# A decoder layer on one core: projections in tiles of 512 tokens, entry normalisation on VectorE alone, stores of normalised tiles moved from SyncE's queue to ScalarE's

## The chip, the cores and the metric

One core of a Trainium2 chip runs the whole program. The metric is the device time of one execution in microseconds (us); lower is better. The engines are TensorE (PE in the rows, its weight loads PEld), VectorE (DVE), ScalarE (ACT), GpSimd (POOL) and SyncE (SP), which here only issues transfers. Each engine takes its instructions in order, and so does each queue of transfers: what stands behind a waiting instruction waits too.

## What is computed

One post-norm decoder layer on 1024 tokens of width 1024, cut to its steps:

```python
h = layer_norm(x, ln_in_g, ln_in_b)                      # entry
proj = h @ w_in                                          # q, k, v of both head groups, 2304 columns
sb = stick_breaking_attention(q_sb, k_sb, v_sb)          # 8 heads of 64, strictly causal
sw = sliding_window_attention(q_sw, k_sw, v_sw, ...)     # 8 heads, 2 key heads, window 128, sinks
merged = concatenate([rms_norm(sb), rms_norm(sw)])
h = layer_norm(ALPHA * h + merged @ w_out, ln1_g, ln1_b)
ffn = (silu(h @ w_gate) * (h @ w_up)) @ w_down           # d_ff = 2816
out = layer_norm(ALPHA * h + ffn, ln2_g, ln2_b)
```

Inputs and outputs are float32. The result must agree with this to a small tolerance.

## The kernel before

**Products in three passes.** A float32 product is made of three matmuls in the type fp32r: each operand is split into a high part (a cast) and a low part (the operand less the cast), and `mm3` (line 178) adds high x high, high x low and low x high in one PSUM bank. So each split costs a cast on ScalarE and a subtraction, on GpSimd for weights (`split_w`, line 114), on VectorE for attention's values (`split_ps`, line 119), on TensorE by a matmul with minus the identity and a second cast for activations (`split_pe`, line 127).

**Entry.** The eight tiles of 128 tokens are loaded (`load_x`, line 263) and normalised (`norm`, line 323, through `ln_apply`, line 156): two `bn_stats` and `bn_aggr` on VectorE, the power for 1/sigma on GpSimd (`rpow`, line 141), then the scaling. Tiles 0 and 1 are scaled by VectorE alone (`fast`: one instruction of 1024 columns, line 159, and two of 512, line 162); for tiles 2 to 7 ScalarE subtracts the mean (line 169), VectorE multiplies (line 170) and GpSimd adds the offset (line 172), each in two halves. A normalised tile is stored to `h_dram` (line 330) and turned on TensorE (`turn_in`, line 332) into the split arrays `xh`, `xl`, four pairs with 256 tokens each. Between the first turns `warm` (line 317) issues 21 matmuls on the identity whose result nobody reads.

**Projections.** `xmul` (line 343) multiplies a strip of 128 weight columns with tokens. In the loop of lines 591 to 604 it runs over `c`, four pieces of 256 tokens, as the tiles arrive: keys, values, two strips of queries, and from the second piece on two blocks of the sliding-window attention (`swa_attend`). Later it takes two pieces at once (`nc_` = 2), still as two runs of 24 matmuls with 256 columns each, one after the other in one PSUM bank: 4 calls in `swa_project` (line 383), 24 in `sb_project` (line 445). Their weights come by `strip` (line 210).

**Around the last projections.** `merge` interleaves attention with projections, and later with the first half of the output projection. Then, for pairs of token tiles in the order 0, 2, 1, 3 (lines 690 to 712), `out_proj` finishes the output projection, `ln_apply` normalises the tile, line 695 stores it to `h1_dram` from SyncE's queue, and `put_b` (line 675) turns it and splits it into the right-hand arrays of the feed-forward part, which is a seven-product scheme (P1 to P7). A tile's `copied` cast is the ScalarE read of its turned data. The loads that `out_proj` needs next (`m`, line 535; `res`, line 631) and the first feed-forward weights (`gr`, `ur`, line 736) stand in SyncE's queue too.

**What sets the order.** A scheduler in the framework orders each engine's instructions from its own model of their times, under the data dependencies and a few added ones: `pe.after(a, b)` puts `a` behind `b` without a wait of its own. So an edit in one place can move instructions elsewhere.

Of the kernel before, what the change touches and what calls it, by code (L numbers as in the profile page):

```python
# [13 lines left out]
F32 = mybir.dt.float32  # L14
# [7 lines left out]
P = 128  # L22
# [59 lines left out]
def layer(ctx: ExitStack, tc: tile.TileContext, x, ln_in, w_sw, w_sb, norm_g,  # L82
# [31 lines left out]
    def split_w(raw, hi, lo):  # L114
        ins = act.copy(hi, raw)  # L115
        pool.tensor_tensor(out=lo, in0=raw, in1=_f(hi), op=ALU.subtract)  # L116
        return ins
# [9 lines left out]
    def split_pe(pending, ps, hi, lo):  # L127

        act.copy(hi, ps)

        def finish():
            pe.matmul(ps, negi, hi, start=False, stop=True, skip_group_check=True)
            act.copy(lo, ps)
        flush(pending)
        pending.append(finish)

# [4 lines left out]
    def rpow(dst, var, scale, eps):  # L141
        dve.tensor_scalar(out=var, in0=var, scalar1=scale, scalar2=eps, op0=ALU.mult, op1=ALU.add)  # L142
        pool.tensor_tensor(out=dst, in0=var, in1=mhalf, op=ALU.pow)  # L143

    def ln_stats(xt, n=2, eps=LN_EPS):
        bst = st.tile([P, n, 6], F32, tag=f"bst{n}", name="bst")
        w, first = D // n, []
        for i in range(n):
            first.append(dve.bn_stats(out=bst[:, i, :], in_=xt[:, i * w:(i + 1) * w]))  # L149
        mv = st.tile([P, 2], F32, tag="mv", name="mv")  # L150
        dve.bn_aggr(out=mv, in_=bst)  # L151
        rstd = st.tile([P, 1], F32, tag="rstd", name="rstd")
        rpow(rstd, mv[:, 1:2], 1.0, eps)
        return mv[:, 0:1], rstd, first
# [36 lines left out]
    for c in range(4):  # L191
        xh.append((c1p, rp)[c // 2].tile([P, KT, 256], F32R, tag="r", name=f"xh{c}"))
        xl.append((c1p, rp)[c // 2].tile([P, KT, 256], F32R, tag="r", name=f"xl{c}"))
# [14 lines left out]
    loaded = []  # L208

    def strip(i, ahead=2):  # L210
        while len(loaded) < min(len(strips), i + ahead):
            i_ = len(loaded)
            raw = w_raw(strips[i_])
            hi, lo = (U([P, KT, P], "whu"), U([P, KT, P], "wlu")) if i_ == 3 else w_tiles()
            for k in (slice(0, 4), slice(4, KT)) if i_ < 2 else (slice(0, KT),):
                ins = split_w(raw[:, k], hi[:, k], lo[:, k])
                if i_ == 0:
                    pe.after(ins, copied)
# [98 lines left out]
    def warm(n):  # L317

        ps = bps.tile([P, P], F32, tag="z", bufs=ZB, name="warm")
        for i in range(n):  # L320
            pe.matmul(ps, negi, negi, start=True, stop=True)

    def norm(t):
        xt = xts[t]
        first, last = ln_apply(xt, xt, g_in, b_in, t < 2)
# [6 lines left out]
    def turn_in(t):  # L332
        xt = xts.pop(t)
        c, o, todo = t // 2, (t % 2) * P, []
        for g in range(2):
# [4 lines left out]
            split_pe(todo, ps, xh[c][:, 4 * g:4 * g + 4, o:o + P], xl[c][:, 4 * g:4 * g + 4, o:o + P])  # L340
        flush(todo)

    def xmul(w, c0, nc_):
        hi, lo = w
        ps = bps.tile([P, nc_, 256], F32, tag="pp", name="pp")
        for h in range(nc_):
            mm3(ps[:, h, :], [(hi[:, k, :], lo[:, k, :], xh[c0 + h][:, k, :], xl[c0 + h][:, k, :])
                              for k in range(KT)])
        return ps.rearrange("p a b -> p (a b)"), slice(c0 * 256, (c0 + nc_) * 256)
# [223 lines left out]
    strip(0, 2)  # L573
    load_x(2)
    load_x(3)
    strip(2, 2)
    for t in range(4, NT):
        load_x(t)
# [5 lines left out]
    pe.on, pe.last = True, None  # L584
    warm(3)
    turn_in(0)
    warm(12)
    turn_in(1)
    warm(6)
    pe.on = False  # L590
# [84 lines left out]
    def put_b(name, src, o):  # L675
# [6 lines left out]
        for hi, k0 in hw:  # L682
            n = hi.shape[1]
            split_pe(todo, ps[:, k0:k0 + n], hi[:, :, o:o + P], lw[0][0][:, k0:k0 + n, o:o + P])
# [3 lines left out]
    hs = {}  # L688
    d0, d1 = slice(0, 512), slice(512, D)
    for n, c in enumerate(order):  # L690
        if n in (1, 2):
            ms[order[n + 1]] = out_load(0, order[n + 1])
        for t, h in out_proj(c, ms[c], wo, load_acc(c, acc_dram), ("z" if n < 3 else "pp", "pp")):
            ln_apply(h, h, g1, b1, True, LN_EPS / ALPHA ** 2)
            sp.dma_start(h1_dram[t], h)
            o = (t % 4) * P
            if t < 4:
                hs[t] = h
                put_b("B11", h[:, d0], o)
                put_b("B21", h[:, d1], o)  # L700
# [7 lines left out]
            put_b("B22", h[:, d1], o)  # L708
# [321 lines left out]
```

## Time and profile before

| | |
|---|---|
| Time, median of 3 runs | 1191.04 us (1190.03 to 1191.77) |
| The profiled execution | 1192.59 us, its span 1190.8 us |
| Mean granted clock of TensorE | 0.988 of full speed |
| Busy in the span: TensorE, VectorE, GpSimd, ScalarE | 96%, 70%, 52%, 49% |
| Matmuls | 6319 |
| Moved by the DMA engines | 140.17 MB, 118 GB/s on average |

The span runs from the program's first instruction to its last; 1.8 us of the execution lie around it. Busy times are shares of the whole span, over stages that differ; a matmul's record begins when it starts and overlaps the next one's, so TensorE's pace is read from the starts of matmuls that follow each other, not from their durations.

### The profile page before, as it was taken

To read this page: it belongs to the slowest core of one execution; us is meant where nothing else is said; L and a number is where in the kernel's file an instruction comes from. 1 tells how busy PE (TensorE), PEld (TensorE's weight loads), DVE (VectorE), ACT (ScalarE), POOL (GpSimd) and SP (SyncE) were. 2 spreads that over 40 slices of the span, in tenths; PEclk is the share of its full clock that TensorE was granted. 3 is DMA by queue.
4 is the path that set the end of the run, shared out by engine and by line. 5 is a ranking of instruction groups with operands and counts; after the bars stand their busy time and mean duration, and the time that the engine had idled before them with its cause. 6 is when DMAs were issued, how large, how long until landed. Compare 5 with 4: busy or idle time off the path is not lost. (4 is left out here: it accounts for less than half of the span.)

```text
span 1190.8 us, 17761 instructions
## 1 busy us (share of the span) xinstructions
PE 1147.4 (96%) x6319; PEld 989.4 (83%) x6319; DVE 836.0 (70%) x1279; ACT 584.5 (49%) x1269; POOL 622.0 (52%) x590
## 2 busy tenths in 40 slices
PE   7799999999999999988999999999999999999996
PEld 5798999999998778866878888888888888888885
DVE  6676687988888887976765546555565448899735
ACT  5566578777777754247423222233323234455531
POOL 5514234757666864334877656676567520000584
PEclk9899999999999999989999999999999999999999
DMA  8302102111104635243333323332233239853431
GB/s 272 144 16 89 32 19 77 31 50 41 50 15 142 217 119 170 106 159 138 119 115 115 107 74 121 116 111 89 84 115 122 82 124 385 328 186 104 129 124 71
DMA packets 59912, 140.17 MB, mean 118 GB/s; under 512 B 7045, under 2 KB 18862, under 8 KB 59824
## 3 DMA queue, kind: packets, MB, share of 16 engines
q1 hardware_dynamic: 45552, 111.24, 29.2%
q10 hardware_dynamic: 14272, 27.81, 6.1%
q8 instruction: 50, 0.82, 0.3%
q14 instruction: 38, 0.31, 0.1%
HBM read 95.23 MB, written 41.17 MB: 115 GB/s over the span
## 5 line engine op out<-in xcount | busy, mean ns | idle before, releaser
L116 POOL TENSOR_TENSOR w<-s,w 128x512 fp32r<-128x512 f32 x88 | 125.5, 1429 | 117.0 <-ACT w L115 117.0
L183 PE MATMUL pp<-xh,whi 128*128 128x256 f32 x544 | 158.6, 292 | 0.0
L183 PE MATMUL pp<-xl,whi 128*128 128x256 f32 x544 | 157.1, 289 | 0.0
L183 PE MATMUL pp<-xh,wlo 128*128 128x256 f32 x544 | 156.8, 289 | 0.0
L115 ACT CAST w<-s 128x512 fp32r<-128x512 f32 x88 | 54.5, 622 | 201.3 <-PE pgu L770 121.6
L843 PE MATMUL pd<-bhl,ahl 128*128 128x512 f32 x612 | 139.2, 389 | 0.0
L843 PEld LDWEIGHTS pd<-bhl,ahl 128*128 128x128 f32 x612 | 114.8, 188 | 24.2 <-DVE bhl L835 0.4
L802 DVE TENSOR_TENSOR t<-t,pgu 128x512 f32<-128x512 f32 x88 | 60.0, 682 | 97.5 <-PE pgu L770 97.3
L481 POOL TENSOR_TENSOR s<-s,s 128x127 f32<-128x127 f32 (+2 forms) x96 | 94.6, 990 | 42.6 <-DVE s L477 20.8
L183 PEld LDWEIGHTS pp<-xh,whi 128*128 128x128 f32 x544 | 106.0, 195 | 1.0 <-issue 0.2
L183 PEld LDWEIGHTS pp<-xl,whi 128*128 128x128 f32 x544 | 105.8, 195 | 0.9
L183 PEld LDWEIGHTS pp<-xh,wlo 128*128 128x128 f32 x544 | 105.5, 194 | 1.0
L835 POOL TENSOR_TENSOR ahl<-ar,ahl 128x512 fp32r<-128x512 f32 x12 | 16.2, 1354 | 134.8 <-ACT ahl L834 134.7
L477 DVE TENSOR_TENSOR_SCAN s<-s,brk 128x128 f32<-128x128 f32 (+1 forms) x64 | 72.8, 1143 | 8.8 <-ACT s L468 8.2
L120 ACT CAST at<-tra 128x256 fp32r<-128x256 f32 (+1 forms) x160 | 55.7, 357 | 44.4 <-DVE at L121 31.6
L834 ACT CAST ahl<-ar 128x512 fp32r<-128x512 f32 x63 | 39.1, 622 | 77.2 <-PE pd L843 47.9
L422 POOL TENSOR_TENSOR L<-L,rd 128x512 f32<-128x512 f32 (+1 forms) x32 | 30.9, 987 | 87.0 <-DVE rd L420 61.1
L121 DVE TENSOR_TENSOR at<-tra,at 128x256 fp32r<-128x256 f32 (+1 forms) x160 | 58.9, 381 | 10.3 <-ACT at L120 8.9
L116 POOL TENSOR_TENSOR w<-gr,w 128x512 fp32r<-128x512 f32 x44 | 62.0, 1419 | 7.6 <-ACT w L115 7.6
L770 PE MATMUL pgu<-B11h,w 128*128 128x512 f32 x176 | 57.9, 390 | 1.6 <-ACT w L115 1.0
L770 PE MATMUL pgu<-T4h,w 128*128 128x512 f32 x176 | 57.9, 390 | 1.5 <-DVE t L802 1.5
L770 PE MATMUL pgu<-T3h,w 128*128 128x512 f32 x176 | 57.9, 390 | 1.0 <-ACT w L115 1.0
(242 smaller groups left out, 3311.8 us busy)
## 6 DMA issues: line engine op xcount, KB each, us to landing
ar<-a_dram SPq DMA_DIRECT2D x73, 256.0 KB, 3.0
a_dram<-act ACTq DMA_DIRECT2D x33, 512.0 KB, 2.6
gr<-in_w_gu SPq DMA_DIRECT2D x24, 512.0 KB, 3.5
ur<-in_w_gu SPq DMA_DIRECT2D x23, 512.0 KB, 3.5
bq<-in_w_down SPq DMA_DIRECT2D x44, 256.0 KB, 5.2
raw<-in_w_sb SPq DMA_DIRECT2D x12, 512.0 KB, 3.4
m<-o_dram SPq DMA_DIRECT2D x32, 128.0 KB, 2.9
res<-h_dram SPq DMA_DIRECT2D x8, 512.0 KB, 5.8
```

What stands on the lines that cost most here:

```text
L115: ins = act.copy(hi, raw)
L116: pool.tensor_tensor(out=lo, in0=raw, in1=_f(hi), op=ALU.subtract)
L120: act.copy(hi, ps)
L121: dve.tensor_tensor(out=lo, in0=ps, in1=_f(hi), op=ALU.subtract)
L183: pe.matmul(ps, a, b, start=(i == 0), stop=(i == n - 1))
L422: pool.tensor_tensor(out=Ls[i], in0=Ls[i], in1=rd[:, 2 * i:2 * i + 2].unsqueeze(2).broadcast_to([P, 2, nk]), op=ALU.mult)
L477: dve.tensor_tensor_scan(s2[:, 0:w][:, ::-1], s2[:, 0:w][:, ::-1], brk[:, 512 - w:][:, ::-1] if last else zero.broadcast_to([P, w]), 1.0 i ...
L481: pool.tensor_tensor(out=s1[:, 0:m], in0=s1[:, 0:m], in1=s2[:, 1:m + 1], op=ALU.mult)
L770: pe.matmul(ps, a, b, start=(start and n == 0), stop=(stop and n == 11), skip_group_check=True)
L802: add = lambda out, x: dve.tensor_tensor(out=out, in0=x, in1=ps, op=ALU.add)
L834: act.copy(w[:, 0], src)
L843: pe.matmul(pd[t], x, y, start=(first and k == 0 and n == 0), stop=(end and k == KF - 1 and n == 2), skip_group_check=True)
```

## The change

It has three parts. (1) `xh` and `xl` become two groups of 512 tokens (each as two tiles of four strips of the contraction), and `xmul` with two pieces issues one run of 24 matmuls with 512 columns in place of two with 256. (2) At the entry all tiles take `ln_apply`'s VectorE form; the `warm` matmuls go; the first two weight strips are loaded ahead of the remaining tiles of `x`, all of `x` is asked for before the next strips, and the first strip's low half is put behind the power of tile 1 on GpSimd. (3) The store of a normalised tile to `h1_dram` is issued from ScalarE's queue, behind the cast of the tile's second `put_b`.

```diff
@@ split_w, split_pe, rpow return their instruction @@
     def split_w(raw, hi, lo):
         ins = act.copy(hi, raw)
-        pool.tensor_tensor(out=lo, in0=raw, in1=_f(hi), op=ALU.subtract)
-        return ins
+        return ins, pool.tensor_tensor(out=lo, in0=raw, in1=_f(hi), op=ALU.subtract)
...
-    for c in range(4):
-        xh.append((c1p, rp)[c // 2].tile([P, KT, 256], F32R, tag="r", name=f"xh{c}"))
-        xl.append((c1p, rp)[c // 2].tile([P, KT, 256], F32R, tag="r", name=f"xl{c}"))
+    for c in range(2):
+        xh.append([(c1p, rp)[c].tile([P, 4, 512], F32R, tag="r", name=f"xh{c}") for g in range(2)])
+        xl.append([(c1p, rp)[c].tile([P, 4, 512], F32R, tag="r", name=f"xl{c}") for g in range(2)])
...
-            raw = w_raw(strips[i_])
+            raw = raws0.pop(0) if raws0 else w_raw(strips[i_])
...
-                ins = split_w(raw[:, k], hi[:, k], lo[:, k])
+                cast, low = split_w(raw[:, k], hi[:, k], lo[:, k])
                 if i_ == 0:
-                    pe.after(ins, copied)
+                    pe.after(cast, copied)
+                    pe.after(low, powers[1])
...
-    def warm(n):
-
-        ps = bps.tile([P, P], F32, tag="z", bufs=ZB, name="warm")
-        for i in range(n):
-            pe.matmul(ps, negi, negi, start=True, stop=True)
-
     def norm(t):
         xt = xts[t]
-        first, last = ln_apply(xt, xt, g_in, b_in, t < 2)
+        first, last = ln_apply(xt, xt, g_in, b_in, True)
...
     def xmul(w, c0, nc_):
         hi, lo = w
-        ps = bps.tile([P, nc_, 256], F32, tag="pp", name="pp")
-        for h in range(nc_):
-            mm3(ps[:, h, :], [(hi[:, k, :], lo[:, k, :], xh[c0 + h][:, k, :], xl[c0 + h][:, k, :])
-                              for k in range(KT)])
-        return ps.rearrange("p a b -> p (a b)"), slice(c0 * 256, (c0 + nc_) * 256)
+        c, o, n = c0 // 2, (c0 % 2) * 256, nc_ * 256
+        ps = bps.tile([P, n], F32, tag="pp", name="pp")
+        mm3(ps, [(hi[:, k, :], lo[:, k, :], xh[c][k // 4][:, k % 4, o:o + n], xl[c][k // 4][:, k % 4, o:o + n])
+                 for k in range(KT)])
+        return ps, slice(c0 * 256, c0 * 256 + n)
...
-    strip(0, 2)
-    load_x(2)
-    load_x(3)
-    strip(2, 2)
-    for t in range(4, NT):
+    raws0 += [w_raw(strips[i]) for i in range(2)]
+    for t in range(2, NT):
         load_x(t)
...
     norm(0)
     norm(1)
-    pe.on, pe.last = True, None
-    warm(3)
+    strip(0, 2)
     turn_in(0)
-    warm(12)
     turn_in(1)
-    warm(6)
-    pe.on = False
+    strip(2, 2)
...
+    def store(t, h, copied):
+
+        pe.after(act.dma_start(h1_dram[t], h), copied)
+
...
             ln_apply(h, h, g1, b1, True, LN_EPS / ALPHA ** 2)
-            sp.dma_start(h1_dram[t], h)
...
-                put_b("B21", h[:, d1], o)
+                store(t, h, put_b("B21", h[:, d1], o))
...
-            put_b("B22", h[:, d1], o)
+            store(t, h, put_b("B22", h[:, d1], o))
```

**How it moves instructions.** First, GpSimd at the entry (`rstd` is the power for a tile's 1/sigma, the second one tile 1's; `wlo`, `wlu` are weights' low parts; `x` a tile of tokens). Before:

```order
L143 TENSOR_TENSOR rstd<-mv,mhalf 128x1
L286 TENSOR_SCALAR nsink<-sink 128x8
L116 TENSOR_TENSOR wlo<-raw,whi 128x512 x4
L143 TENSOR_TENSOR rstd<-mv,mhalf 128x1
L116 TENSOR_TENSOR wlo<-raw,whi 128x1024
L143 TENSOR_TENSOR rstd<-mv,mhalf 128x1
L116 TENSOR_TENSOR wlu<-raw,whu 128x1024
L172 TENSOR_TENSOR x_203<-x_203,b_in 128x512 x2
```

and now:

```order
L143 TENSOR_TENSOR rstd<-mv,mhalf 128x1
L289 TENSOR_SCALAR nsink<-sink 128x8
L143 TENSOR_TENSOR rstd<-mv,mhalf 128x1
L116 TENSOR_TENSOR wlo<-raw,whi 128x512 x4
L143 TENSOR_TENSOR rstd<-mv,mhalf 128x1 x2
L116 TENSOR_TENSOR wlo<-raw,whi 128x1024
L116 TENSOR_TENSOR wlu<-raw,whu 128x1024
L143 TENSOR_TENSOR rstd<-mv,mhalf 128x1 x4
```

The second power has moved ahead of four weight subtractions, and GpSimd's additions to `x` are gone; ScalarE's `L169` instructions are gone with them.

Second, SyncE's queue around the normalised tiles of the last stage (`h_dram_108` to `115` are the eight tiles of `h1_dram`, `m` and `res` the loads of `out_proj`, `gr` the first feed-forward weights). Before:

```order
L695 DMA h_dram_112<-res 128x1024
L695 DMA h_dram_113<-res 128x1024
L535 DMA m<-o_dram_92 128x256
L535 DMA m<-o_dram_93 128x256
L535 DMA m<-o_dram_94 128x256
L535 DMA m<-o_dram_95 128x256
L631 DMA res<-acc_dram_102 128x1024
```

and now:

```order
L622 DMA res<-acc_dram_105 128x1024
L532 DMA m<-o_dram_92 128x256
L532 DMA m<-o_dram_93 128x256
L532 DMA m<-o_dram_94 128x256
L532 DMA m<-o_dram_95 128x256
L622 DMA res<-acc_dram_102 128x1024
```

The four loads of `m` for the last piece stood behind the stores of tiles 0, 1, 4 and 5 and no longer do; in the same way the first `gr` loads stood behind those of tiles 2, 3, 6 and 7.

Third, TensorE at the turns of tiles 4 and 5 (`trh` is turned data, with `ident` a turn, with `negi` the subtraction of a high part; `pc` is the output projection). Before:

```order
L125 MATMUL trh<-ident,res 128x128 x4
L125 MATMUL trh<-ident,tt 128x128 x7
L132 MATMUL trh<-B22h,negi 128x512
L125 MATMUL trh<-ident,tt 128x128
L125 MATMUL trh<-ident,res 128x128 x4
L183 MATMUL pc<-woh,whi 128x512
L183 MATMUL pc<-wol,whi 128x512
L183 MATMUL pc<-woh,wlo 128x512
```

with nine more `pc` behind them, and now:

```order
L124 MATMUL trh<-ident,res 128x128 x4
L124 MATMUL trh<-ident,tt 128x128 x8
L124 MATMUL trh<-ident,res 128x128 x4
L131 MATMUL trh<-B22h,negi 128x512
L131 MATMUL trh<-T2h,negi 128x512 x2
L124 MATMUL trh<-ident,tt 128x128 x4
L131 MATMUL trh<-T1h,negi 128x512
L131 MATMUL trh<-T3h,negi 128x512
```

The twelve `pc` that stood among these turns have moved ahead of them; the next `pc` now come only after the turns of both tiles.

## Rows read from the trace of the kernel before

**Rows 1.** Busy time by stage (windows): stretch, length, each engine (instructions), clock, DMA, GB/s.
```profile
0.00:60.00 60.00, 46.98 (x232) 37.30 (x233) 39.70 (x76) 31.65 (x60) 35.06 (x34) 0.91 0.60 206
120.00:380.00 260.00, 258.39 (x2073) 251.01 (x2072) 213.48 (x372) 191.93 (x495) 144.16 (x197) 1.00 0.16 46
480.00:560.00 80.00, 73.07 (x362) 57.90 (x361) 62.48 (x100) 38.61 (x79) 29.66 (x25) 0.96 0.36 127
```

**Rows 2.** Timeline of PE, projections: start, duration, instruction (second: 24th after the first).
```profile
130.66 0.28 PE L183 MATMUL pp<-xh,whi 128*128 128x256 f32 x1
...
133.53 0.28 PE L183 MATMUL pp<-xh,whi 128*128 128x256 f32 x1
```

**Rows 3.** Timeline of PE, output projection (second: 13th after the first).
```profile
495.17 0.39 PE L183 MATMUL pc<-woh,wlo 128*128 128x512 f32 x1
...
498.12 0.39 PE L183 MATMUL pc<-woh,whi 128*128 128x512 f32 x1
```

**Rows 4.** Timeline of all engines, entry; in brackets idle time before, and what ended it.
```profile
7.71 1.29 DVE L159 SCALAR_TENSOR_TENSOR x<-x,mv,g_in 128x1024 f32<-128x1024 f32 x1 [1.86 <-ACT g_in L282]
...
11.96 5.94 POOL L116 TENSOR_TENSOR wlo<-raw,whi 128x512 fp32r<-128x512 f32 x4 [1.63 <-ACT whi L115]
...
13.35 0.15 DVE L142 TENSOR_SCALAR mv<-mv 128x1 f32<-128x1 f32 x1
...
17.85 0.57 POOL L143 TENSOR_TENSOR rstd<-mv,mhalf 128x1 f32<-128x1 f32 x1
18.46 1.41 DVE L162 SCALAR_TENSOR_TENSOR x<-x,rstd,b_in 128x512 f32<-128x512 f32 x2 [2.92 <-POOL rstd L143]
...
26.35 0.52 PE L183 MATMUL pp<-xl,whi 128*128 128x256 f32 x1
...
35.43 0.33 ACTq L330 DMA_DIRECT2D h_dram<-x  x1
35.80 0.37 ACT L370 COPY vr<-pp 128x256 f32<-128x256 f32 x1 [3.21 <-POOL x L172]
...
41.06 0.80 PE L132 MATMUL trx<-xh,negi 128*128 128x512 f32 x1 [4.25 <-ACT xh L129]
```

**Rows 5.** Windows of 4 us at the entry, columns as in rows 1.
```profile
34.00:38.00 4.00, 0.95 (x6) 0.32 (x4) 4.00 (x5) 0.37 (x1) 4.00 (x3) 0.80 0.32 131
...
42.00:46.00 4.00, 4.00 (x21) 4.00 (x21) 3.09 (x4) 2.75 (x7) 2.71 (x4) 0.50 0.52 201
```

**Rows 6.** Groups of VectorE by line and shape, first 62 us: busy us, mean ns, idle before.
```profile
L170 DVE SCALAR_TENSOR_TENSOR x<-x,rstd,g_in 128x512 f32<-128x512 f32 x12 | 15.8, 1366 | 0.8 <-ACT x L169 0.8
L159 DVE SCALAR_TENSOR_TENSOR x<-x,mv,g_in 128x1024 f32<-128x1024 f32 x2 | 3.4, 1703 | 1.9 <-ACT g_in L282 1.9
L162 DVE SCALAR_TENSOR_TENSOR x<-x,rstd,b_in 128x512 f32<-128x512 f32 x4 | 2.9, 750 | 4.3 <-POOL rstd L143 2.9 <-ACT b_in L282 1.4
```

**Rows 7.** Waits of SyncE's queue, 440 to 560 us: total us, times, longest.
```profile
SPq L695 <- DVE res L162: 34.1, 6, 8.9
...
SPq L695 <- DVE at L121: 10.1, 1, 10.1
```

**Rows 8.** Timeline of SyncE's queue, 440 to 560 us.
```profile
507.61 2.09 SPq L535 DMA_DIRECT2D m<-o_dram  x4
...
542.91 1.15 SPq L736 DMA_DIRECT2D gr<-in_w_gu  x2
```

**Rows 9.** Timeline of VectorE, 480 to 560 us; idle time before it in brackets.
```profile
513.22 1.23 DVE L538 TENSOR_TENSOR wlo<-m,whi 128x1024 fp32r<-128x1024 f32 x1 [3.59 <-ACT whi L537]
```

**Rows 10.** Windows of 4 us in the last stage before the feed-forward part.
```profile
520.00:524.00 4.00, 4.00 (x11) 3.11 (x10) 2.68 (x6) 0.00 (x0) 1.97 (x2) 0.50 0.05 22
...
540.00:544.00 4.00, 3.66 (x17) 2.16 (x17) 3.56 (x6) 4.00 (x11) 1.03 (x1) 1.00 0.18 73
```

**Rows 11.** Waits of PE, 480 to 612 us: total us, times, longest.
```profile
PE pgu L770 <- ACT w L115: 2.0, 2, 1.0
```

**Rows 12.** Transfers by line: size, median us from issue to landing.
```profile
res<-h_dram SPq DMA_DIRECT2D x8, 512.0 KB, 5.8
```

More of the change, by code (lines that the diff above doesn't have):

```diff
@@ L127, in split_pe @@
     def split_pe(pending, ps, hi, lo):
-        act.copy(hi, ps)
+        copied = act.copy(hi, ps)
         def finish():
@@ L135, in split_pe @@
         pending.append(finish)
+        return copied
     def flush(pending):
@@ L142, in rpow @@
         dve.tensor_scalar(out=var, in0=var, scalar1=scale, scalar2=eps, op0=ALU.mult, op1=ALU.add)
-        pool.tensor_tensor(out=dst, in0=var, in1=mhalf, op=ALU.pow)
+        return pool.tensor_tensor(out=dst, in0=var, in1=mhalf, op=ALU.pow)
+    powers = []
     def ln_stats(xt, n=2, eps=LN_EPS):
@@ L152, in ln_stats @@
         rstd = st.tile([P, 1], F32, tag="rstd", name="rstd")
-        rpow(rstd, mv[:, 1:2], 1.0, eps)
+        powers.append(rpow(rstd, mv[:, 1:2], 1.0, eps))
         return mv[:, 0:1], rstd, first
@@ L207, in layer @@
     strips = [w_sw[s] for s in (4, 5, 0, 1, 2, 3)] + [w_sb[w * 4 + p] for p in range(NPAIR) for w in range(3)]
-    loaded = []
+    loaded, raws0 = [], []
     def strip(i, ahead=2):
@@ L333, in turn_in @@
         xt = xts.pop(t)
-        c, o, todo = t // 2, (t % 2) * P, []
+        c, o, todo = t // 4, (t % 4) * P, []
         for g in range(2):
@@ L339, in turn_in @@
                 turn(ps, i, xt[:, k * P:(k + 1) * P])
-            split_pe(todo, ps, xh[c][:, 4 * g:4 * g + 4, o:o + P], xl[c][:, 4 * g:4 * g + 4, o:o + P])
+            split_pe(todo, ps, xh[c][g][:, :, o:o + P], xl[c][g][:, :, o:o + P])
         flush(todo)
@@ L683, in put_b @@
             n = hi.shape[1]
-            split_pe(todo, ps[:, k0:k0 + n], hi[:, :, o:o + P], lw[0][0][:, k0:k0 + n, o:o + P])
+            copied = split_pe(todo, ps[:, k0:k0 + n], hi[:, :, o:o + P], lw[0][0][:, k0:k0 + n, o:o + P])
+        return copied
     order = (0, 2, 1, 3)
```

## The prediction

> **What bounds the kernel now.** I read the busy times by stage first, then the starts of matmuls, then what each engine waited for where TensorE was not full. TensorE is full over the projections and attention (258.39 of 260 us [rows 1]), so there its instructions are the time; it was busy for only 46.98 of the first 60 us and for 73.07 of the 80 us before the feed-forward part. In the feed-forward part, which the change leaves alone, it is full again. So the change can gain in three places: by cheaper instructions where TensorE is full, and by fewer waits in the two stages where it is not.
>
> **Wider matmuls.** TensorE's price of a matmul is the distance of starts. With 256 columns, (133.53 - 130.66) / 24 = 0.1196 us [rows 2]; with 512 and the same type, (498.12 - 495.17) / 13 = 0.2269 us [rows 3]. Two of the first cost 0.2392 us, so a pair that becomes one saves 0.0123 us. The change merges the matmuls of 4 calls in the second group's queries and 24 in the stick-breaking projections: 28 calls of 48, 1344 matmuls, 672 pairs. 672 x 0.0123 = 8.3 us. They lie where TensorE is full, so nearly all of it counts; the lower end is 6.2 us, three quarters, if attention's waits on VectorE (213 of 260 us busy there [rows 1]) take a quarter back. I take 8. The loop over four pieces keeps its 256 columns and saves nothing.
>
> The Trainium skill ("TensorE: Matmul & The Clock Gate", section "Back-to-back issue gap") prices a matmul at full clock at its columns over 2.4 GHz plus about 2.5 ns. By that a pair would save 2.5 ns, an estimate of 1.7 us in all; the rows show 12.3 ns, five times as much, and I go by the rows.
>
> **The entry.** The rows tell a chain [rows 4]. Tile 1's variance is ready at 13.35 + 0.15 = 13.5 us, but GpSimd is at four weight subtractions from 11.96 for 5.94 us, so the power runs at 17.85, VectorE waits 2.92 us and the tile is done at 18.46 + 1.41 = 19.87. Now the power stands ahead of the subtractions: it runs at 13.5 to 14.1. VectorE's 1024-column step takes 1.3 us [rows 4] to 2.1 (with 1703 ns as the mean of the two, the other is 2.1), the two halves 0.75 to 1.37 us each, the low value alone, the high one beside a busy GpSimd [rows 6]: done by 16.3 to 17.4. From there to steady projection matmuls took 26.35 - 19.87 = 6.5 us, because ScalarE did weight casts and mean subtractions between the casts that TensorE waited for. In the new order it has only the casts: the turns, two casts of 0.6 us and two subtractions on TensorE, together about 2.8 us, so the projections start near 20.2 in place of 26.35: **6.1 us** (4 if the weights' low parts, which now end 5.94 us after 14.1, at 20.0 and not at 17.9, hold the first matmuls).
>
> Next, TensorE stood still around 34 to 41 us, busy 0.95 of 4 us [rows 5]. A cast waited 3.21 us for GpSimd's addition to `x`, by way of a store in ScalarE's queue, and TensorE 4.25 us for a cast of turned data [rows 4]; with the wait for the copied values that was 6.1 us. That cast stood behind the keys' casts, which waited for VectorE, held by normalisation steps at 1366 ns in place of some 700. GpSimd's additions, which made these slow, are gone, so the chain is gone but for one wait of 1 to 1.5 us: **4.9 us** (at least 2). The granted clock then stood at 0.50, the 1.2 GHz level, in 42 to 46 us, after the engine had stood still: 21 matmuls there where 33 fit at rows 2's pace, 1.5 us. I count that only in the upper end. The removal of the 21 idle matmuls I price at nothing: with them the projections' first steady matmul still took 0.52 us [rows 4] where later ones take 0.28 [rows 2], so they had not bought the higher level; if they had a use, losing it costs such a 1.5 us, which lies inside the ends.
>
> VectorE's own load does not grow: six tiles had two steps of 1366 ns, 2.73 us each; now they have one of 1.3 and two of 0.75, 2.8 us, as GpSimd is mostly idle then. But it stands in one queue with the keys' and queries' subtractions, for which TensorE's banks wait: **-1.5 us**. Sum 6.1 + 4.9 - 1.5 = 9.5 us; the low ends give 4 + 2 - 1.5 = 4.5, the high ones 6.1 + 6.1 + 1.5 = 13.7. ScalarE's stores of tiles 2 to 7 stay where they were, 0.33 us each [rows 4]. The loads of `x` and the second pair of strips change places in SyncE's queue: three tiles of `x`, 1.5 MB, now go first, 7 us at the stage's 206 GB/s [rows 1]. The strips are wanted only when 48 matmuls of keys and values are done, at 20.2 + 48 x 0.12 = 26 us or later, which I take as cover; if it is gone, up to those 7 us less what the earlier start gives are paid.
>
> **The stores.** SyncE's queue stood 34.1 + 10.1 us before the eight stores, for tiles that were not ready [rows 7]. Behind the first four, `m` for the last piece was asked for only at 507.61, behind the other four the first feed-forward weights only at 542.91 [rows 8]. The first made VectorE, the busiest engine just then, wait 3.59 us for a cast of `m` [rows 9], and TensorE behind it: 11 matmuls in 520 to 524 us at a granted 0.50, the 1.2 GHz level, after it had stood still [rows 10], where they need 11 x 0.227 = 2.5 us at the higher level: 1.5 us. The second made the first feed-forward matmuls wait 2.0 us for casts of weights [rows 11]. If all goes: 3.6 + 1.5 + 2.0 = 7.1 us. Against it: twelve output matmuls, 12 x 0.227 = 2.7 us, which filled the turns of tiles 4 and 5, now run ahead of them, so TensorE waits there for ScalarE's casts; and ScalarE is full at the end (4.00 of 4 us [rows 10]), where four of its eight new issues of 0.33 us lie: 1.4 us. 7.1 - 2.7 - 1.4 = **3.0 us**. The ends: 7.1 at best; at worst nothing is gained, both costs are paid and the other four issues too, -5.
>
> The Trainium skill ("DMA: Bandwidth & Descriptors", section "Issuing engines are not separate DMA queues") says that a second issuing engine saves only the sequencer's time for the issue. Here that would be eight times a third of a microsecond on SyncE, which bounds nothing, so this part would bring nothing; the rows show a queue held by its order, which that sentence does not speak of.
>
> **Sum.** 8.0 + 9.5 + 3.0 = 20.5 us. The profiled execution took 1192.6 us (span 1190.8), so it would take 1172.1; it lies 1.55 us above the median of the runs, 1191.0, so the median becomes **1170.5 us**. Lower ends: 6.2 + 4.5 - 5 = 5.7 us, 1185; upper ends: 8.3 + 13.7 + 7.1 = 29.1 us, 1162. The forecast as a whole: 0.62.
>
> **Rivals.**
> - *VectorE bounds the entry.* If its steps are slow for another reason than GpSimd, a tile costs 2.1 + 2 x 1.37 = 4.8 us in place of 2.73, over six tiles 12.6 us, and the entry's gain is gone: 1191 - 11 = 1180. For it: 39.70 of 60 us busy there. Against: rows 6 show 750 and 1366 ns for the same work without and with GpSimd. 0.12.
> - *The pace goes with the columns.* If the extra 12 ns of the narrow matmul come from what runs beside it and not from each instruction, the first part brings some 2 us in place of 8: 1176.5. This is what the skill's formula says; rows 2 and 3 speak against it. 0.08.
> - *The stores were hidden anyway.* If the loads behind them wait for SBUF space just as long, the third part brings nothing: 1173.5. For it: loads of `m` and weights reuse space that the last turns free. 0.08.
> - *ScalarE's queue is held by the stores* (slower). A transfer issued there may first wait for an earlier one to land, 5.8 us for a large one [rows 12], with casts queued behind it that TensorE needs. Four of eight such waits cost 23 us, over the 17.5 of the other two parts: 1196.5. It decides from 17.5 / 8 = 2.2 us per store on. Against: the stores' data are ready when the cast ahead of them is done. 0.05.
> - *The scheduler's new order loses elsewhere* what the parts gain, as a wait in the attention: no change 0.03, slower 0.02.
>
> **The numbers.** Faster 0.62 + 0.12 + 0.08 + 0.08 = 0.90; the same within 0.2% (2.4 us, about what a measurement of this kernel can tell from no change) 0.03; slower by more 0.07. The range from 1162 to 1185 takes in the bounds of the sum and the three rivals that are faster, and leaves the last two out; some of the forecast's own mass lies outside too, so 8 in 10 is in it.
>
> **What would show it.** In the profile after: 6319 - 672 - 21 = 5626 matmuls, the wide ones of the projections at 0.227 us from start to start; tile 1 done by 17.4 us and projections running by 20.5; no still stretch of over 2 us between 34 and 41; TensorE's busy time in the first 60 us near 55; `m` for the last piece asked for before tile 5 is done, and no 3.6 us wait of VectorE for it; the first `gr` issued ahead of the last turn. Wrong would be: VectorE at 1.2 us or more for 512 columns in the entry, ScalarE idle before a store, or the turns of tiles 4 and 5 leaving TensorE at the 1.2 GHz level for more than 5 us.

## The result, and the profile after

The changed kernel takes **1212.44 us** (median of 4 runs, 1209.76 to 1213.89); the kernel before, beside it on the same chip, 1191.05 (1190.03 to 1191.77). The ratio is 1.0179, 95% interval 1.0167 to 1.0191: 21 us slower, where 20.5 us faster was forecast. The profiled execution has a span of 1208.0 us.

By stage (windows: stretch, length, busy us and instructions of PE, PEld, DVE, ACT, POOL, granted clock, DMA share, GB/s), with the lines that answer to [rows 1]:

```profile
0.00:60.00 60.00, 47.12 (x265) 36.51 (x266) 49.32 (x88) 28.97 (x63) 23.36 (x22) 0.94 0.57 208
120.00:380.00 260.00, 250.01 (x1330) 209.72 (x1330) 195.19 (x344) 182.40 (x457) 133.47 (x176) 0.97 0.17 51
480.00:560.00 80.00, 69.08 (x352) 55.47 (x352) 64.55 (x114) 35.84 (x74) 27.47 (x30) 0.93 0.38 135
```

TensorE, full in the projections and the attention before (258.39 of 260 us [rows 1]), now leaves 10 us open there. The third window has 4 us less of TensorE's time than before, but it holds another piece of the work, since the stages have shifted: up to 504 us it is still attention. In the entry's first 60 us TensorE is busy for 47.12 us in place of 46.98, with 265 matmuls in place of 232 (21 of which were the idle ones); some 55 us had been forecast.

Single events of the trace tell when the time went. The table has the first or last start of a kind of matmul, in us (its last row goes to that matmul's end); *fillers* are the projections' and the output projection's matmuls, which the program puts between those of the attention.

| | before | after |
|---|---|---|
| first projection matmul | 23.5 | 19.3 |
| first turn of a stick-breaking weight (`tra`) | 206.3 | 200.0 |
| last projection matmul | 381.4 | 356.1 |
| last `tra` | 480.8 | 504.1 |
| last matmul of the output projection (`pc`) | 536.0 | 551.7 |
| first feed-forward matmul (`pgu`) | 548.6 | 567.7 |
| from there to the last matmul | 633.3 | 631.4 |

So the new kernel is 6 us ahead at 200 us and 25 us ahead with its last projection, and 19 us behind when the feed-forward part starts. The attention took 304.1 us from first to last `tra`, 274.5 before. The stage behind it, from the last `tra` to the first `pgu`, is no longer than it was, 63.6 us and 67.8 before; it holds 108 `pc` and 150 before, as more of them ran in the attention. The attention is the same work for VectorE, ScalarE and GpSimd, and its matmuls are the same too; all that changed in it is the width of its fillers and the order.

The order moved by itself. A scheduler decides for each engine what stands next (its settings are untouched by the change). TensorE's matmuls from the 40th to the 61st `tra`, as kind, columns and count, first before and then after (`pp` are the projections, `z` the attention's scores, `av` its weights times the values, `pv` turns of values):

```
tra128x3 pp256x10 z384x2 pp256x6 tra128x3 pp256x3 av256x1 pp256x2 z512x2 av256x4 tra128x4 av256x3 z512x2 pv128x4
  pp256x10 tra128x4 av256x1 pp256x2 z512x2 av256x3 pp256x5 av256x1 pp256x7 av256x1 av128x2 tra128x4 z128x2 pp256x14
  tra128x3 pp256x5 av256x1 pp256x3 av256x3 pp256x1 av256x1 pp256x1 z256x2
tra128x3 z384x2 pv128x4 pp512x1 tra128x3 pp512x13 av256x1 pp512x3 z512x2 pp512x1 av256x3 z512x2 av256x1 pp512x1 tra128x4
  av256x3 tra128x4 pp512x17 av256x1 pp512x2 z512x1 av256x3 z512x1 z128x1 av256x1 z128x1 av256x1 av128x2 tra128x7
  pp512x21 av256x1 pp512x1 av256x4 z256x1
```

The same piece of attention held 69 narrow projection matmuls, at 0.1196 us 8.3 us [rows 2], and now holds 60 wide ones, at 0.2269 us 13.6 us, most of them in three blocks of 13, 17 and 21. The fillers are both coarser and used up faster. In the executed profiles, between the first and the last `tra`, they stood in 176 pieces (runs of fillers with nothing else between; median 0.48 us; 38% of their time in pieces of over 2 us) before, and in 100 pieces (median 1.15 us, 73%) after.

What this does shows in two sets of windows, of the kernel before first and of the one after in the second fence:

```profile
200.00:240.00 40.00, 39.01 (x310) 37.70 (x309) 34.02 (x54) 31.58 (x78) 29.57 (x41) 1.00 0.18 51
240.00:280.00 40.00, 39.39 (x316) 37.90 (x316) 35.34 (x54) 28.91 (x75) 24.26 (x35) 1.00 0.18 54
280.00:320.00 40.00, 40.00 (x323) 39.07 (x322) 34.73 (x56) 31.01 (x75) 26.43 (x41) 1.00 0.13 37
356.00:380.00 24.00, 24.00 (x194) 23.42 (x194) 20.23 (x31) 17.93 (x44) 14.22 (x22) 1.00 0.36 111
```

```profile
200.00:240.00 40.00, 39.87 (x212) 33.36 (x211) 28.88 (x47) 27.87 (x68) 23.37 (x35) 1.00 0.17 48
240.00:280.00 40.00, 39.90 (x222) 34.12 (x221) 29.21 (x47) 26.71 (x65) 23.41 (x30) 1.00 0.14 43
280.00:320.00 40.00, 38.75 (x221) 32.96 (x219) 30.48 (x48) 28.44 (x71) 24.11 (x35) 1.00 0.14 44
356.00:380.00 24.00, 20.03 (x84) 15.22 (x83) 20.18 (x32) 17.02 (x39) 18.41 (x23) 0.72 0.53 165
```

From 200 to 320 us TensorE is full in both, so nothing looks wrong there. But VectorE, which the attention needs most, works 28.88 + 29.21 + 30.48 = 88.6 us in place of 34.02 + 35.34 + 34.73 = 104.1: TensorE is full of fillers while the attention waits. After 356 us the projections are gone and the attention left over has little to hide its waits. A closer look at that place, windows of 4 us:

```profile
360.00:364.00 4.00, 2.78 (x12) 1.89 (x12) 4.00 (x8) 3.95 (x11) 3.83 (x5) 0.72 0.59 196
364.00:368.00 4.00, 3.15 (x9) 2.02 (x9) 3.94 (x7) 3.95 (x8) 3.40 (x7) 0.50 0.37 95
368.00:372.00 4.00, 2.30 (x7) 1.81 (x8) 4.00 (x5) 2.47 (x6) 3.92 (x3) 0.50 0.31 111
372.00:376.00 4.00, 4.00 (x16) 3.43 (x15) 3.51 (x7) 2.13 (x5) 2.46 (x3) 0.57 0.52 137
```

VectorE is now full, TensorE waits for it, and having stood still gets the clock of 1.2 GHz (0.50) for what it does run. Waits of TensorE from 356 to 500 us, the three largest (total us, times, longest); all of them add up to 15.8 us, before 6.6 from 356 to 480:

```profile
PE tra L500 <- DVE at L120: 6.6, 7, 1.6
PE av L512 <- DVE at L120: 2.5, 3, 1.3
PE pc L185 <- DVE var L550: 1.8, 1, 1.8
```

The clock adds to this. The mean granted clock from 356 us to the end of the attention was 0.99 before (first line) and is 0.92 now:

```profile
356.00:481.00 125.00, 118.07 (x702) 102.02 (x702) 102.40 (x162) 78.78 (x176) 80.64 (x102) 0.99 0.50 165
356.00:505.00 149.00, 132.51 (x686) 109.03 (x685) 125.79 (x200) 88.08 (x203) 96.89 (x129) 0.92 0.41 138
```

**The entry** shows an old wait at a new place. Timeline of the engines after 24 us (start, duration, instruction, idle time ahead of it and its releaser):

```profile
26.22 2.34 POOL L116 TENSOR_TENSOR wlo<-raw,whi 128x1024 fp32r<-128x1024 f32 x1
26.28 5.58 DVE L164 SCALAR_TENSOR_TENSOR x<-x,rstd,b_in 128x512 f32<-128x512 f32 x2 [0.45 <-POOL rstd L143]
28.52 2.78 POOL L116 TENSOR_TENSOR wlu<-raw,whu 128x1024 fp32r<-128x1024 f32 x1
31.89 0.33 ACTq L327 DMA_DIRECT2D h_dram<-x  x1
32.26 0.36 ACT L352 CAST kd<-pp 64x256 fp32r<-64x256 f32 x1 [6.71 <-DVE x L164]
33.66 0.80 PE L131 MATMUL trx<-xh,negi 128*128 128x512 f32 x1 [6.73 <-ACT xh L128]
```

VectorE's pair, 2 x 0.75 us when alone [rows 6], takes 5.58 us, about as long as GpSimd's two weight subtractions beside it (5.1 us, from 26.22 to 31.30). ScalarE's store of that tile waits for VectorE, ScalarE's casts stand behind the store for 6.71 us, and TensorE behind a cast for 6.73: more than the 4.25 us before it that were to go [rows 4].

**The last stage.** `m` for the last piece is still waited for, and the first feed-forward weights are asked for 22 us ahead of the first feed-forward matmul at 567.7 (5.7 us before [rows 8]); VectorE's wait and SyncE's issue in the timeline:

```profile
530.12 1.23 DVE L535 TENSOR_TENSOR wlo<-m,whi 128x1024 fp32r<-128x1024 f32 x1 [4.54 <-ACT whi L534]
```

```profile
545.63 3.98 SPq L732 DMA_DIRECT2D gr<-in_w_gu  x2
```

### The profile page after: what moved, and what is told of

It is laid out like the page before. It is cut to its first block, busy times and chain, and to the rows that moved or that the text cites. A ratio compares the mean times of both kernels' runs of the same rounds, so it can differ in the third digit from the quotient of the medians.

```text
span 1208.0 us, 16351 instructions
## 1 busy us (share of the span) xinstructions
PE 1148.7 (95%) x5626; PEld 953.5 (79%) x5626; DVE 831.3 (69%) x1279; ACT 579.3 (48%) x1257; POOL 600.0 (50%) x578
## 5 line engine op out<-in xcount | busy, mean ns | idle before, releaser
L116 POOL TENSOR_TENSOR w<-s,w 128x512 fp32r<-128x512 f32 x88 | 122.6, 1397 | 119.5 <-ACT w L115 119.4
L185 PE MATMUL pp<-xh,whi 128*128 128x512 f32 (+1 forms) x320 | 118.0, 369 | 1.2 <-DVE q L361 1.2
L185 PE MATMUL pp<-xl,whi 128*128 128x512 f32 (+1 forms) x320 | 116.9, 365 | 0.0
L185 PE MATMUL pp<-xh,wlo 128*128 128x512 f32 (+1 forms) x320 | 116.7, 365 | 0.0
L478 POOL TENSOR_TENSOR s<-s,s 128x127 f32<-128x127 f32 (+2 forms) x96 | 90.6, 946 | 49.0 <-ACT s L466 18.5
L474 DVE TENSOR_TENSOR_SCAN s<-s,brk 128x128 f32<-128x128 f32 (+1 forms) x64 | 66.0, 1038 | 16.4 <-ACT s L465 15.9
L185 PEld LDWEIGHTS pp<-xh,whi 128*128 128x128 f32 x320 | 61.4, 192 | 9.3 <-DVE q L361 1.5
L185 PEld LDWEIGHTS pp<-xl,whi 128*128 128x128 f32 x320 | 61.3, 192 | 7.9 <-ACT xl L132 0.2
L185 PEld LDWEIGHTS pp<-xh,wlo 128*128 128x128 f32 x320 | 61.1, 191 | 8.1
L766 PE MATMUL pgu<-T2h,w 128*128 128x512 f32 x176 | 57.9, 389 | 0.0
```

The costliest lines, as they stand in the source:

```text
L116: return ins, pool.tensor_tensor(out=lo, in0=raw, in1=_f(hi), op=ALU.subtract)
L185: pe.matmul(ps, a, b, start=(i == 0), stop=(i == n - 1))
L474: dve.tensor_tensor_scan(s2[:, 0:w][:, ::-1], s2[:, 0:w][:, ::-1], brk[:, 512 - w:][:, ::-1] if last else zero.broadcast_to([P, w]), 1.0 i ...
L478: pool.tensor_tensor(out=s1[:, 0:m], in0=s1[:, 0:m], in1=s2[:, 1:m + 1], op=ALU.mult)
L766: pe.matmul(ps, a, b, start=(start and n == 0), stop=(stop and n == 11), skip_group_check=True)
```

## Experiments

Three theories: **order** (the wide call makes the scheduler place fillers coarser and sooner, and this is the loss); **wide matmuls** (512 columns hold TensorE or a bank for longer, and that hurts the attention in any order); **entry and stores** (the other two parts do the harm).

### One part at a time

`e1_widths`: the layout and the widths of the change alone, in the kernel before.

> The kernel before with the new layout of the normalised tokens and the 512-column projections alone; entry and stores as before. Order theory (a projection call of 24 matmuls in place of 48 makes the scheduler run the projections ahead of the attention, so that the last attention units have nothing to fill them): in the written order the last projection now stands ahead of 141 attention transposes, before ahead of 91, so this kernel is slower than before by itself: 1205 to 1220 us, with PE's lost time from 300 us on up by about 25 us. Rival, the entry and the stores do the harm: 8 us faster than before, 1183 us (1180 to 1186).

`e3_entry`: the new entry alone.

> The kernel before with the new entry alone (all tiles normalised by VectorE, raw weights loaded ahead, normalised tiles 2 and later stored as before, no warm-up matmuls, no fixed order); layout, widths and h1 stores as before. Order theory: the entry is worth the 5 us that TensorE's lost time over the first 60 us fell by, 1186 us (1183 to 1191). Rival, the entry and the stores do the harm: slower than before, over 1197.

`e4_stores`: the stores' new place alone.

> The kernel before with the stores of the normalised tiles of the last projection issued from ScalarE's queue alone. Order theory: within 3 us of before, 1188 to 1194. Prediction on record: 3 us faster, 1188. Rival, the stores do the harm through ScalarE's queue or the last pieces: 1196 or more.

Measured: e1_widths 1212.06 us, ratio 1.019 (1.0168 to 1.0212); e3_entry 1191.9, 1.0015 (1.0002 to 1.0027); e4_stores 1192.71, 1.0012 (1.0002 to 1.0021). The first part alone loses as much as the whole change, and the other two by themselves change little, both a trifle to the slower side. e1 changes the layout of `xh` and `xl` together with the width; which of the two moves the order was not run apart. In e1 the last projection matmul starts at 361.8 us, the last `tra` at 507.3, and VectorE falls as after: 89.5 us of the 120 from 200 us, 88.6 after and 104.1 before (part of this is e1's later first `tra`, at 213.3). The order of e3 had moved as well (its last projection call stands behind 178 `tra` in place of 189), so the entry's worth had to be asked again below. Nor do the parts simply add up: from the last `tra` to the first `pgu`, with 108 `pc` in either, the whole change takes 63.6 us and e1 58.6. No run holds the order of that stretch, so what the 5 us are stays open.

In e4 the stores do what the diff says: the first gate weights are issued at 528.14 us and not at 542.91 [rows 8]. Yet the wait for `m` is 3.28 us where it was 3.59 [rows 9]. Its load is issued at 504.83 us, 2.8 ahead of before, of which 1.8 is the lead that this execution has anyway at the last `tra`: with the stores out of its way, the load waits for the `pr` matmul that reads an earlier `m`. The lines: the first issue of gate weights, VectorE's wait, SyncE's wait for that matmul (total us, times, longest):

```profile
528.14 4.22 SPq L742 DMA_DIRECT2D gr<-in_w_gu  x2
```

```profile
511.07 1.23 DVE L539 TENSOR_TENSOR wlo<-m,whi 128x1024 fp32r<-128x1024 f32 x1 [3.28 <-ACT whi L538]
```

```profile
SPq L536 <- PE pr L551: 28.3, 1, 28.3
```

The first feed-forward matmuls no longer wait for casts of weights (2.0 us before [rows 11]). But TensorE's turns now wait 4.0 us for VectorE where they waited 2.1; the longest of these waits, 2.21 us, is new and stands among the last turns, and around it TensorE runs at 1.2 GHz in a stretch where it had a clock of 1.00 [rows 10]:

```profile
540.90 1.09 PE L125 MATMUL trh<-ident,tt 128*128 128x128 f32 x4 [2.21 <-DVE tt L711]
```

```profile
540.00:544.00 4.00, 3.04 (x10) 2.27 (x11) 3.90 (x8) 1.67 (x3) 0.00 (x0) 0.50 0.02 5
```

### Holding the fillers back

`e2_widths_held`: the first matmul of a filler call held behind an earlier `tra`.

```
+        return first
...
+    def hold(first, lag):
+        if len(tras) >= lag:
+            pe.after(first, tras[-lag])
...
+                            tras.append(pe.transpose(ps[:, j, :], A[:, j * P:(j + 1) * P], ident))
```

> The same as e1_widths, but the first matmul of each projection call and of each out-projection piece is held behind the attention transpose that was written 18 ahead of it, which brings the order back to that of before (out-projection pieces behind transposes 208, 216, 220, 220, 229, as before). Order theory: the loss is gone and the gain of the width stays, 1183 us (1179 to 1188). Rival, the wide matmuls themselves hurt the attention (a call holds TensorE or its bank for longer): as slow as e1_widths, 1205 to 1220. Rival of the entry and the stores: 1183, as e1_widths.

Measured: 1229.42 us, 1.0317 (1.0293 to 1.034): a miss for the order theory in the form that I gave it. The fillers did run out as late in the order as before (the last projection matmul stands behind 197 `tra` in both; it starts at 419.1 us, 381.4 before), but TensorE now stood idle in the middle. Windows and waits of 200 to 360 us:

```profile
200.00:240.00 40.00, 34.59 (x172) 28.30 (x171) 26.00 (x44) 24.21 (x60) 22.45 (x30) 0.91 0.12 37
```

```profile
PE tra L513 <- DVE at L123: 6.8, 7, 1.7
PE av L524 <- ACT at L122: 3.1, 4, 1.1
PE tra L513 <- POOL s L483: 2.8, 2, 1.4
```

The pieces had stayed coarse: 93 of them, 69% of their time in pieces of over 2 us. While a piece runs, VectorE and ScalarE finish and wait; when it is over, TensorE runs a few attention matmuls and then waits for them. So either the grain counts and not the pace, or the wide matmuls themselves hurt. The next two kernels tell these apart.

### The order alone, and the width alone

`e5_widths_order_of_before`: e1 with every engine's instructions up to the end of the attention chained in the order of before. `e6_narrow_order_of_widths`: the kernel before with its 256-column matmuls, chained in the order of e1.

```
+ORDER_PE = """
...
+    for eng, ordered in ((pe, ORDER_PE), (act, ORDER_ACT), (dve, ORDER_DVE), (pool, ORDER_POOL), (sp, ORDER_SP)):
...
+        for a, b in zip(todo_, todo_[1:]):
+            pe.after(eng.log[b][1], eng.log[a][1])
```

> The 512-column projections and their layout as in e1_widths, but every engine's instructions up to the last matmul of the attention stage are chained in the order in which the kernel before has them; each 512-column matmul stands where the first of a pair of 256-column matmuls of the same call stood. Only the widths then differ from before. Order theory: the loss of e1_widths was its order, fine fillers turned into coarse ones that run ahead; here it is gone and the width's 8 us are left: 1183 us (1180 to 1187). Rival, the wide matmuls themselves hurt the attention: 1205 to 1220, as e1_widths and e2_widths_held.

> The reverse: the kernel before with its 256-column projections, all engines chained in the order of e1_widths; two 256-column matmuls stand where one of 512 stood. Order theory: before's time plus the loss of the order plus nothing gained from the width, 1220 us (1212 to 1226). Rival, the wide matmuls themselves hurt: 1191 (1188 to 1195).

Measured: e5 1189.17 us, 0.9992 (0.9978 to 1.0005); e6 1216.9 us, 1.0223 (1.0199 to 1.0247). This settles it: the wide matmuls in the old order lose nothing, and the narrow ones in the new order lose 26.8 us. In the new order, e1 against e6, the width is worth 1216.9 - 1212.1 = 4.8 us. The windows of e6 show the loss without any wide projection matmul: in the 40 us from 280 us TensorE is busy for 39.20 and VectorE for 27.03, 34.73 before:

```profile
280.00:320.00 40.00, 39.20 (x325) 38.52 (x323) 27.03 (x49) 25.63 (x69) 21.80 (x32) 1.00 0.15 44
```

But e5 gains 1 us (-0.6 to 2.6) and not the 8 expected. In its trace the first `tra` is 2.6 us ahead of before, the last projection matmul 5.6, the last `tra` 3.9, the last `pc` 1.0. So most of the 8.3 us is there at 376 us; behind that the stages end with waits for other engines, and TensorE, after one of them at 504 us, runs at a mean clock of 0.84 in this stretch (first fence before, second e5):

```profile
500.00:520.00 20.00, 16.40 (x79) 12.62 (x79) 15.70 (x28) 9.84 (x19) 5.60 (x6) 0.94 0.45 154
```

```profile
500.00:520.00 20.00, 15.85 (x69) 12.13 (x69) 13.84 (x26) 9.79 (x18) 6.59 (x6) 0.84 0.41 132
```

`e9_widths_spread`: e1 with a filler call spread over the attention by a rule, no table of the order.

```
+    def mm3(ps, ops, spread=None):
...
+        i, at = 0, len(tras) - LAG
...
+                if spread and at + i // spread >= 0:
+                    pe.after(ins, tras[min(at + i // spread, len(tras) - 1)])
```

> e1_widths with every second matmul of a projection or out-projection call held behind one more attention transpose, so that a call is spread over the attention; by the written order the fillers then stand in 118 pieces in place of 94, 45 per cent of them in pieces of over 2 us (e1_widths 67, e2_widths_held 69, before 36), and run out behind transpose 204 as before. Coarse-grain theory (long pieces of filler in front of attention work that is ready): between e2_widths_held and e5_widths_order_of_before, 1195 to 1210 us. Rival, only the place where the fillers run out counts: 1183 to 1190.

Measured: 1197.02 us, 1.005 (1.003 to 1.0071), in the range of the coarse-grain theory. The four kernels with wide matmuls, from their profiles:

| | pieces of filler | median us | share in pieces over 2 us | last projection matmul, us | time, us |
|---|---|---|---|---|---|
| e5, order of before | 163 | 0.68 | 35% | 375.8 | 1189.2 |
| e9, spread | 119 | 0.97 | 46% | 384.0 | 1197.0 |
| e1, free | 95 | 1.23 | 68% | 361.8 | 1212.1 |
| e2, held | 93 | 0.93 | 69% | 419.1 | 1229.4 |

The two with coarse fillers are the slow ones, whether the fillers end early (e1) or late (e2), and e9, whose fillers are finer, lies between them and e5. The grain is not all, though: e1 and e2 are equally coarse and 17 us apart. From 200 to 356 us TensorE is busy for 151.3 us in e1 and for 138.0 in e2, so holding whole calls back costs something of its own.

### What the other parts are worth when the order stays

The same chain, from the end of the entry to the end of the attention, in the whole change (`e7_change_order_of_before`) and in the new entry alone (`e8_entry_order_of_before`, which keeps the new layout with matmuls of 256 columns):

> The whole change (widths, entry, stores), with every engine's instructions from the end of the entry to the end of the attention chained in the order of before. Order theory: what the parts are worth without the order, the 5 us of the entry and some of the width's (1 to 5 us as e5_widths_order_of_before), stores near nothing: 1184 us (1179 to 1189). Rival, the parts' gains don't add, since a wait further on takes the entry's gain back: 1189 to 1193.

> The new entry alone, chained behind the entry in the order of before. Order theory: 1186 us (1183 to 1189), the 5 us by which TensorE's lost time of the first 60 us fell, which e3_entry lost again to its own order. Rival, the entry's gain is taken back further on whatever the order: 1189 to 1193.

Measured: e7 **1184.72 us, 0.9947 (0.9928 to 0.9966)**; e8 1188.67, 0.9974 (0.9959 to 0.9989). So the change in the old order is 6.6 us faster than before, not 21 slower, and the entry brings 2.7 of it (1.3 to 4.9 by the interval), less than the 5 that I expected. The profiled executions are kinder, 6.9 us ahead at the first `tra` in e8; one execution differs from the next by some us here (e8 1185.41 to 1190.35).

Three variants of e7. `e12_stores_on_sync` puts the stores back:

> e7_change_order_of_before with the stores of the normalised tiles of the last projection back on SyncE's queue. Prediction on record for the stores: 3 us slower than e7, 1188. Theory from e4_stores (1.4 us slower for the stores alone): within 2 us of e7, 1183 to 1187, since the turns of tiles 4 and 5 lose on TensorE what the earlier loads win.

Measured: 1185.1 us, 0.994 (0.9919 to 0.9961), the same as e7 (1184.72) within some 3 us, by the two intervals. No run shows a gain by the stores, and e4 alone was slower by 0.2 to 2.5 us.

`e10_low_parts_on_vector` moves the two weight subtractions from GpSimd to VectorE:

```
-    def split_w(raw, hi, lo):
+    def split_w(raw, hi, lo, eng=pool):
...
+                cast, low = split_w(raw[:, k], hi[:, k], lo[:, k], dve if i_ in (2, 3) else pool)
```

> e7_change_order_of_before with the low parts of weight strips 2 and 3 subtracted on VectorE in place of GpSimd. In e7 the second half of tile 3's normalisation took 5.6 us on VectorE beside GpSimd's two 1024-column subtractions, and ScalarE stood behind its store for 5.4 us. Theory, GpSimd's subtractions hold VectorE up and everything behind it in the entry: the pair takes 1.4 to 1.6 us, TensorE's stretch without work after 26 us shrinks by 2 to 4 us, and the time falls by as much, 1181 us (1178 to 1184). Rival, the store at the head of ScalarE's queue or a load sets that wait: 1184 to 1187.

`e11_low_parts_and_late_stores` also writes the tile's store behind its casts:

```
-        (act if t > 1 else sp).dma_start(h_dram[t], xt)
...
+        if t > 1:
+            pe.after(act.dma_start(h_dram[t], xt), copied)
```

> e10_low_parts_on_vector and the stores of the normalised tiles 2 and later written behind the casts of their own turns, so that no cast stands behind a store that waits for VectorE. Theory of VectorE: at most 1 us better than e10, 1180 us (1177 to 1184). Rival, the store sets the wait: 2 to 5 us better than e10.

Measured: e10 1182.24 us, 0.9932 (0.9919 to 0.9945); e11 **1180.7 us, 0.992 (0.9902 to 0.9938)**, the fastest of all, 10 us under before. Timeline of e10 at the place where VectorE's pair took 5.62 us in e7:

```profile
26.33 1.42 DVE L280 SCALAR_TENSOR_TENSOR x<-x,rstd,b_in 128x512 f32<-128x512 f32 x2 [0.45 <-POOL rstd L259]
...
28.14 0.37 ACT L468 CAST kd<-pp 64x256 fp32r<-64x256 f32 x1 [1.93 <-DVE x L280]
...
28.86 1.21 DVE L232 TENSOR_TENSOR wlo<-raw,whi 128x1024 fp32r<-128x1024 f32 x1
29.98 1.22 DVE L232 TENSOR_TENSOR wlu<-raw,whu 128x1024 fp32r<-128x1024 f32 x1
```

The pair is down from 5.62 to 1.42 us; the two subtractions take 2.4 us on VectorE where GpSimd took 5.1; ScalarE's idle time ahead of its casts falls from 5.37 to 1.93 us. TensorE's longest wait of the entry, in e7 and then in e10:

```profile
PE trx L247 <- ACT xh L244: 4.7, 1, 4.7
```

```profile
PE trx L247 <- ACT xh L244: 2.7, 3, 1.8
```

So VectorE, held up beside GpSimd, was the root of that wait. What this is worth in time is less sure: the medians fall by 2.5 us and by 1.5 more in e11, but e10 against e7 and e11 against e10 lie within their intervals, and e11 against e7 just at the edge (its upper end 0.9938, e7's middle 0.9947).

## Why the prediction was wrong

**The step that failed** is in the first part: the saved pitch lies "where TensorE is full, so nearly all of it counts". TensorE was full because a scheduler put just so much filler between the steps of the attention, and with the first part it places other pieces. I took the order of before as given and held a loss by the new one for a rival of 0.05 in all, without a price; the order as written told it beforehand: 69 narrow against 60 wide matmuls for the same piece of attention. What it costs is measured: 26.8 us with the widths of before (e6), and 1212.1 - 1189.2 = 22.9 us with the new ones (e1 against e5). How the scheduler reckons was not part of the runs; that it is the order and not the width is.

- **Widths, -8.0.** The pitch was right: in the profile after, from 121.90 to 125.30 us, 16 wide matmuls start at a distance of (125.30 - 121.90) / 15 = 0.2267 us, as in [rows 3], and their number, 5626 in all, was right. Their worth was 1 us in the order of before by e5, 4.0 by e7 against e8 (which differ beside the widths in the stores alone, without a gain in any run), and 4.8 in the new order, and not 8. The last two are each uncertain by 3 to 4 us, from the intervals of their two kernels; e5's, up to 2.6, leaves out my lower end of 6.2. The first and the last of the 16 lines:

```profile
121.90 0.39 PE L185 MATMUL pp<-xh,whi 128*128 128x512 f32 x1
...
125.30 0.39 PE L185 MATMUL pp<-xh,whi 128*128 128x512 f32 x1
```

- **The pace goes with the columns**: the rows decide against it, as the pair became 0.012 us cheaper. The Trainium skill ("TensorE: Matmul & The Clock Gate", section "Back-to-back issue gap") gives the formula behind this rival as the gap of an isolated matmul, which the prediction does not say.
- **The entry, -9.5.** It brought 2.7 us (e8). The earlier start came: the first projection matmul at 19.3 us and an unbroken run of them from 20.5 (20.2 forecast), tile 1 done at 17.7 (17.4 at the latest; the prediction's own slow steps, 13.5 + 2.1 + 2 x 1.37, add up to 18.3). The term of 4.9 for the wait at 34 to 41 us failed. The wait left that place (TensorE busy 3.50 of 34 to 38 us), but "GpSimd's additions, which made these slow, are gone, so the chain is gone" was wrong: GpSimd's weight subtractions took the additions' place, and one wait of 6.7 us stands at 27 to 34. The price of such a step, "0.75 to 1.37 us each", was 2.8 beside a weight subtraction. The 1.37 is a mean over steps beside GpSimd and steps without it; the trace of before has one beside a weight subtraction, at 2.28:

```profile
22.91 2.37 POOL L116 TENSOR_TENSOR wlu<-raw,whu 128x1024 fp32r<-128x1024 f32 x1
23.55 2.28 DVE L170 SCALAR_TENSOR_TENSOR x<-x,rstd,g_in 128x512 f32<-128x512 f32 x1 [0.80 <-ACT x L169]
```

  In the profile after, each half of the pair ended some 0.55 us behind one of GpSimd's subtractions: the first at 29.11 (28.56), the second, in the line below, at 31.86 (31.30). Without the subtractions the pair was 1.42 us long (e10).

```profile
29.04 2.82 DVE L164 SCALAR_TENSOR_TENSOR x<-x,rstd,b_in 128x512 f32<-128x512 f32 x1
```

  The Trainium skill ("SBUF — State Buffer", section "Summary: rules for kernel authors") says that of a VectorE instruction with two SBUF inputs and a GpSimd instruction that reads SBUF the one issued second blocks until the other is done. The trace agrees with it in these ends, and by that rule the subtractions would have been priced beside the norm's scaling steps. The rival *VectorE bounds the entry* was half right: the bound, but for GpSimd's sake and not for another reason (e10).
- **The stores, -3.0.** No gain (e12, e4). The step that failed is that the stores held the load of `m`: in e4, without them, it waits 28.3 us for an earlier `m` to be read, and VectorE's wait of 3.6 us stays at 3.3. For `m` the rival *The stores were hidden anyway* came true with its mechanism. The feed-forward weights did come 15 us earlier in e4, and the 2.0 us wait for their casts went, but TensorE's longer waits for VectorE at the last turns and the clock of 0.50 there stand against it; no run takes the two apart. In the profile after TensorE is at 0.56 to 0.59 over 8 us behind the turns of tiles 4 and 5, as the prediction's sign of being wrong has it; but before it stood at 0.71, 0.50 and 0.94 in the three windows from 516 us, so that stretch is not new and tells nothing about the stores:

```profile
532.00:536.00 4.00, 2.46 (x9) 1.97 (x10) 4.00 (x8) 2.66 (x6) 2.00 (x2) 0.56 0.52 178
536.00:540.00 4.00, 4.00 (x12) 3.09 (x12) 4.00 (x10) 0.00 (x0) 2.94 (x3) 0.59 0.59 196
```

- **ScalarE's queue is held by the stores**, the slower rival: not by these stores. But a store ahead of casts did hold ScalarE in the entry, 6.71 us, by waiting for its data and not for an earlier transfer; I had left those as "where they were".

Still open is where in each stage the rest of the width's 8 us goes in the order of before. The trace of e5 shows 5.6 us at the last projection and 1 at the last output matmul, with waits and a lower clock between; no run takes these apart. Open too are how the scheduler comes to its order and whether the layout has a part in it.

## What to carry to other kernels

Where a scheduler fills the waits of one chain with another chain's instructions, the size of an instruction can change the order: before costing a wider instruction, compare the new order with the old at a few places (how many us of filler stand between two steps of the other chain, and in how large pieces), and where it has moved, pin the old order to see what the edit itself is worth. A full engine is not proof that its work is the right work: look at whether the engines of the other chain have become emptier. And when a wait is to go, ask which other instruction of the engine that caused it will stand at that place next.

## What the runs showed of the hardware

- Two 512-column steps of VectorE (`scalar_tensor_tensor`, three operands read) took 5.58 us while GpSimd ran subtractions of 1024 columns, and 1.42 us without; each ended some 0.55 us behind one of the subtractions. GpSimd's power of 128x1 took 1.53 us at 20.04 us of the changed kernel, beside a VectorE step of 1024 columns, and 0.57 before with no such step beside it [rows 4].
- The same subtraction of 128x1024 took 2.34 to 2.78 us on GpSimd and 1.21 on VectorE.
- TensorE's granted clock fell to 0.50, its level of 1.2 GHz, after stretches in which it had waited (364 to 372 us after), and that adds to the price of a wait: in the 4 us from 364 it was busy for 3.15 us with 9 matmuls.
